# First norm of a hybrid layer: context's norm, scales and softplus queue issued behind the image's, first head's value products ahead of the context's products

## The chip, the cores and the metric

The kernel runs on one core of a Trainium2 chip. The metric is the device time of one execution in microseconds (us), here the median over runs. The engines are TensorE (PE, with its weight loads as PEld), VectorE (DVE), ScalarE (ACT), GpSimd (POOL) and SyncE (SP), which issues the DMAs.

## What is computed

One layer over 512 image tokens and 256 context tokens of 1024 channels. The part in question is its start:

```python
sc, scc = silu(c), silu(c_ctx)
mod_x = sc @ mod_w + mod_b            # shift, scale, gate: image
mod_c = scc @ mod_w + mod_b           # the same for the context
hx = modulate(rms_norm(x, norm1_g), sh1x, sc1x)
hc = modulate(rms_norm(ctx, norm1_g), sh1c, sc1c)
px, pc = split_proj(hx @ w_in), split_proj(hc @ w_in)
ret_c, ret_x = retention_mixer(pc, px, ret_decay, rows)      # 4 heads, q, k of 128, v of 256
lru_c, lru_x = lru_mixer(pc[4], px[4], conv_w, conv_b, lru_wa, lru_ba, lru_wx, lru_bx, lru_lambda)
```

The retention needs log_sigmoid(ret_decay) and the recurrent mixer softplus(-lru_lambda). After it come gates, an output projection, a second norm, a feed-forward over 16384 single-neuron experts and a last norm; the change does not touch them.

## The kernel before

Channels lie on the 128 partitions in eight chunks k, tokens in the free dimension: xT is the image (8 chunks of 128x512), cT the context (128x256). A float32 product is made of three products of rounded parts (mm3, L63 to 67: L65 is high by high, L66 and L67 take one low part each); split (L60 to 62) makes the parts, the high one on ACT, the low one on DVE. In names an h or l at the end is the high or low part.

The first norm, L169 to 284. inv_rms (L174) squares the chunks on ACT, adds them up on DVE (ssq), sums over the partitions by one product with ones, and takes scale, root and reciprocal (L184 to 186). The shift and scale of a chunk k come from mod_rows1 (L198; PE, eight products of 256 columns and two transposes, for image and context at once) where k is below NROW = 4, and otherwise from mod_dots (L210; DVE, two products of 128x1024 with crow, for the image, and two more later for the context). normed (L218) makes xn on DVE, the high part hh or ch on ACT and the low part hl or cl on DVE. The image's chunks go in the order of KORD, and with each, PE adds its share to four projections: outs0 = pu, p5, pk, pq, of which pu and pk have 768 columns (image and context) in a slot of 1024, p5 and pq 512. PSUM has three slots of 1024 and two of 512, and these are all of it: whatever comes later waits until a slot is read out. Then stand in the program the softplus queue (L245 to 277: 24 columns, some 30 small DVE operations), the context's mod_dots, norm and chunks.

Head 0 follows. Context products of pu (proj_ctx), lru_in (L301 to 321: u from pu by ACT and six DVE taps, x5 from p5 and its gelu g5), context products of pk, rope_split of pk and pq; lru_scan (L324: four gate products pg, their tanh as roots or gi on ACT, then exp, tanh, square, root and the scans on DVE); and in head() the value products pv (six token tiles t, each 24 products of 256 columns), their mean vm and the parts vh and vl (L411 to 426), and scores pS, weights P and outputs po (L428 to 443). A head has two recurrent chunks: the second's pu and p5 come behind the first's lru_scan.

The order in which an engine takes its instructions is fixed when the program is built, by a scheduler that goes by readiness on its own model and by the order in the source; a slot of a pool that is still in use makes the next user wait for the last reader.

Of the kernel before, what the change touches and what calls it, by code (L numbers as in the profile page):

```python
# [44 lines left out]
NROW = 4  # L45
# [7 lines left out]
def block_kernel(ctx: ExitStack, tc: tile.TileContext, A):  # L53
# [118 lines left out]
    rstd = st.tile([128, NT], F32, name="rstd")  # L172

    def inv_rms(src, o, n):  # L174
        ps = psum(n if n == NX else D, name="ps_ss")
        ssq = st.tile([128, NX], F32, name="ssq")
        S.activation(ssq[:, :n], src[:, 0], AF.Square)
        for k in range(1, KT):
            sq = st.tile([128, NX], F32, name="sq", bufs=2)
            S.activation(sq[:, :n], src[:, k], AF.Square)  # L180
            V.tensor_tensor(ssq[:, :n], ssq[:, :n], sq[:, :n], op=OP.add)
        PE.matmul(ps[:, :n], onesf, ssq[:, :n], start=True, stop=True)
        r = rstd[:, o:o + n]
        V.tensor_scalar(r, ps[:, :n], 1.0 / D, EPS, op0=OP.mult, op1=OP.add)  # L184
        S.activation(r, r, AF.Sqrt)
        V.reciprocal(r, r)


    def mod_load(k):
        if k < NROW:  # L190
            mw = st.tile([128, KT, 256], F32, name="mw", bufs=2)
            SY.dma_start(mw, A["mod_a"][k])
        else:
            mw = st.tile([128, 2, D], F32, name="mwc", bufs=4)
            SY.dma_start(mw, A["mod_c"][k - NROW])
        return mw
# [53 lines left out]
    sp_z = const.tile([128, 24], F32, name="sp_z")  # L250
    sp_q = const.tile([128, 24], F32, name="sp_q")
    S.activation(sp_w, spin, AF.Abs)
    S.activation(sp_w, sp_w, AF.Exp, scale=-1.0)
    V.tensor_scalar(sp_z, sp_w, 2.0, None, op0=OP.add)
    V.reciprocal(sp_z, sp_z)
    V.tensor_tensor(sp_z, sp_z, sp_w, op=OP.mult)
    V.tensor_tensor(sp_q, sp_z, sp_z, op=OP.mult)
    V.memset(sp, 1.0 / 19)
    for n in range(8, -1, -1):
        V.tensor_tensor(sp, sp, sp_q, op=OP.mult)  # L260
        V.tensor_scalar(sp, sp, 1.0 / (2 * n + 1), None, op0=OP.add)
    V.scalar_tensor_tensor(sp, sp, 2.0, sp_z, op0=OP.mult, op1=OP.mult)
    V.tensor_scalar(sp_w, spin, -1.0, 0.0, op0=OP.mult, op1=OP.max)
    V.tensor_tensor(sp, sp, sp_w, op=OP.add)
    sp4 = const.tile([128, 16], F32, name="sp4")
    V.tensor_scalar(sp4, sp[:, 0:16], 4.0, None, op0=OP.mult)
    nsp4 = const.tile([128, 16], F32, name="nsp4")
    V.tensor_scalar(nsp4, sp[:, 0:16], -4.0, None, op0=OP.mult)
    hb = const.tile([128, 32], F32, name="hb")
    V.tensor_scalar(hb, col("ba", 0, 32), 0.5, None, op0=OP.mult)  # L270
    epsc = const.tile([128, 1], F32, name="epsc")
    V.memset(epsc, EPS)
    lgam = const.tile([128, 8], F32, name="lgam")
    V.tensor_scalar(lgam, sp[:, 16:24], -1.0, None, op0=OP.mult)
    nlgam = sp[:, 16:24]
    lg768 = const.tile([128, 4], F32, name="lg768")
    V.tensor_scalar(lg768, lgam[:, 4:8], 768.0, None, op0=OP.mult)
# [776 lines left out]
```

## Time and profile before

| | us |
|---|---|
| median of 3 runs (1873.9 to 1877.84) | 1876.19 |
| profiled execution, its own time | 1879.51 |
| its span | 1877.7 |
| PE busy (97% of the span) | 1820.2 |
| DVE busy (81%) | 1512.3 |
| ACT busy (44%) | 824.3 |
| mean granted clock of PE | 0.99 |

Busy time is the sum of an engine's instructions in the one profiled execution; a wait is idle time just before an instruction, put down to what ended it. A granted clock of 1.00 is 2.4 GHz, 0.50 is 1.2 GHz. In names of the views digits of buffers are left out: p is p5.

### The profile page before, as it was taken

How to read it: one execution, taken by the hardware profiler on the slowest of the kernel's cores; microseconds unless marked ns; L12 is line 12 of the kernel's file. 1: busy time of each engine (PE TensorE's matmuls, PEld its weight loads, DVE VectorE, ACT ScalarE, POOL GpSimd, SP SyncE). 2: the span in 40 equal slices, each digit the busy share in tenths (PEclk: the TensorE clock that was granted, in tenths of full speed). 3: DMA queues.
4: the chain of work that ended last, by engine and by line, in shares of the span. 5: the costliest groups of instructions: out<-in, count | busy, mean ns of one | idle time of the engine just before them, and what ended most of it. 6: DMA issues, size and time to landing. Idle time of an engine off the chain costs nothing.

```text
span 1877.7 us, 26999 instructions
## 1 busy us (share of the span) xinstructions
PE 1820.2 (97%) x9969; PEld 1603.0 (85%) x9969; DVE 1512.3 (81%) x2801; ACT 824.3 (44%) x1213; POOL 375.7 (20%) x327
## 2 busy tenths in 40 slices
PE   7899999999999999999999999999999999999997
PEld 3788888887888989999999988888887888888885
DVE  8987878788844579999988578886786879788688
ACT  4667575765222444445545333333333333333333
POOL 0000000000000000000022134443443535445350
PEclk9999999999999999999999999999999999999999
DMA  7122121225943433567778999998989999999986
GB/s 310 52 67 68 57 68 57 68 64 189 335 136 115 138 108 115 184 193 238 261 283 299 317 345 328 345 336 298 323 324 312 346 340 337 347 331 355 319 302 208
DMA packets 175753, 432.72 MB, mean 230 GB/s; under 512 B 14082, under 2 KB 87170, under 8 KB 171140
## 3 DMA queue, kind: packets, MB, share of 16 engines
q1 hardware_dynamic: 138756, 296.75, 46.7%
q0 software_dynamic: 36864, 134.23, 19.7%
q8 instruction: 78, 1.28, 0.3%
q14 instruction: 55, 0.45, 0.1%
HBM read 389.32 MB, written 41.62 MB: 229 GB/s over the span
## 4 chain that ended last, share of the span: by engine, by line
PE 74%; DVE 11%; DMA 9%; ACT 3%; issue 2%; SPq 1%; DVEq 0%; ACTq 0%
PE po L65 8%; PE po L66 8%; PE po L67 8%; PE pS L65 7%; PE pS L66 7%; PE pS L67 7%; DMA wt<-wd 4%; DMA vw<-in_v_dram 2%; DVE wl L62 2%; PE pgm L65 1%; PE pgm L66 1%; PE pgm L67 1%; PE pmm L66 1%; PE pmm L67 1%; PE pmm L65 1%
## 5 line engine op out<-in xcount | busy, mean ns | idle before, releaser
L61 ACT ACTIVATE wh<-w 128x1024 fp32r<-128x1024 f32 (+1 forms) x216 | 224.8, 1043 | 369.0 <-DMA w<-in_uT_dram 105.0
L65 PE MATMUL pS<-h2h,wh 128*128 128x384 f32 x1024 | 347.1, 339 | 7.0 <-ACT gt L756 6.7
L67 PE MATMUL pS<-h2h,wl 128*128 128x384 f32 x1024 | 346.1, 338 | 0.7 <-DVE wl L62 0.7
L66 PE MATMUL pS<-h2l,wh 128*128 128x384 f32 x1024 | 346.2, 338 | 0.0
L62 DVE TENSOR_TENSOR wl<-w,wh 128x1024 fp32r<-128x1024 f32 (+1 forms) x216 | 259.0, 1200 | 88.2 <-ACT wh L61 87.5
L801 POOL DMA_INDIRECT row<-in_u_dram,ei x128 | 181.9, 1421 | 609.7 <-DVE row L803 316.0
L66 PE MATMUL po<-vwl,ah 128*128 128x512 f32 x768 | 299.9, 391 | 1.2 <-DVE vwl L62 1.2
L67 PE MATMUL po<-vwh,al 128*128 128x512 f32 x768 | 298.9, 390 | 0.0
L65 PE MATMUL po<-vwh,ah 128*128 128x512 f32 x768 | 271.5, 395 | 10.0 <-ACT vwh L61 8.1
L61 ACT ACTIVATE ah<-af 128x384 fp32r<-128x384 f32 x128 | 67.2, 525 | 387.0 <-PE po L66 220.2
L809 POOL DMA_INDIRECT row<-in_v_dram,ei x128 | 183.9, 1436 | 208.5 <-DVE acc L814 175.2
L65 PEld LDWEIGHTS pS<-h2h,wh 128*128 128x128 f32 x1024 | 193.2, 189 | 14.3 <-ACT gt L756 8.4
L67 PEld LDWEIGHTS pS<-h2h,wl 128*128 128x128 f32 x1024 | 193.1, 189 | 6.0 <-DVE wl L62 1.0
L66 PEld LDWEIGHTS pS<-h2l,wh 128*128 128x128 f32 x1024 | 193.3, 189 | 4.3
L62 DVE TENSOR_TENSOR vwl<-vw,vwh 128x1024 fp32r<-128x1024 f32 x128 | 156.1, 1220 | 27.1 <-ACT vwh L61 25.6
L65 PEld LDWEIGHTS po<-vwh,ah 128*128 128x128 f32 x768 | 143.1, 188 | 38.4 <-ACT vwh L61 10.6
L814 DVE SCALAR_TENSOR_TENSOR acc<-row,act,acc 128x1024 f32<-128x1024 f32 x127 | 162.7, 1281 | 14.0 <-DMA row<-in_v_dram,ei 13.4
L66 PEld LDWEIGHTS po<-vwl,ah 128*128 128x128 f32 x768 | 144.4, 188 | 29.9 <-DVE vwl L62 2.3
L67 PEld LDWEIGHTS po<-vwh,al 128*128 128x128 f32 x768 | 144.4, 188 | 27.8 <-DVE al L62 0.2
L61 ACT ACTIVATE vwh<-vw 128x1024 fp32r<-128x1024 f32 x128 | 134.4, 1051 | 61.6 <-DMA vw<-in_v_dram 59.9
L803 DVE SCALAR_TENSOR_TENSOR row<-row,h2t 128x1024 f32<-128x1024 f32 x128 | 153.8, 1220 | 2.4 <-DMA row<-in_u_dram,ei 2.4
L62 DVE TENSOR_TENSOR al<-af,ah 128x384 fp32r<-128x384 f32 x128 | 71.0, 554 | 62.6 <-ACT ah L61 57.5
(372 smaller groups left out, 3505.8 us busy)
## 6 DMA issues: line engine op xcount, KB each, us to landing
w<-in_uT_dram SPq DMA_DIRECT2D x128, 512.0 KB
vw<-in_v_dram SPq DMA_DIRECT2D x128, 512.0 KB
w<-in_w_in_dram SPq DMA_DIRECT2D x48, 512.0 KB
wd<-stg SPq DMA_DIRECT2D x24, 1024.0 KB
modb<-in_mod_t_dram SPq DMA_DIRECT2D x32, 512.0 KB
wt<-wd SPq DMA_DIRECT2D x9, 1536.0 KB
gd<-gt SPq DMA_DIRECT2D x57, 192.0 KB
gr<-gd SPq DMA_DIRECT2D x57, 192.0 KB
```

Source lines behind the costliest of these rows:

```text
L61: S.activation(hi, src, AF.Copy)
L62: V.tensor_tensor(lo, src, f(hi), op=OP.subtract)
L65: PE.matmul(out, wh, xh, start=start, stop=False)
L66: PE.matmul(out, wh, xl, start=False, stop=False)
L67: PE.matmul(out, wl, xh, start=False, stop=stop)
L801: G.indirect_dma_start(out=row, out_offset=None, in_=A["u"], in_offset=bass.IndirectOffsetOnAxis(ap=ei[:, j:j + 1], axis=0))
L803: V.scalar_tensor_tensor(row, row, 1.0, h2t, op0=OP.mult, op1=OP.mult, accum_out=act[:, j:j + 1])
L809: G.indirect_dma_start(out=row, out_offset=None, in_=A["v"], in_offset=bass.IndirectOffsetOnAxis(ap=ei[:, j:j + 1], axis=0))
L814: V.scalar_tensor_tensor(acc, row, act[:, j:j + 1], acc, op0=OP.mult, op1=OP.add)
```

## The change

NROW is 3: chunk 3 too gets its shift and scale by dot products. The norm's sum of squares is done on PE alone, eight products with a matrix of 1/1024 for each source, and the root takes its epsilon as a bias; the image's sum lies in p5's bank, the context's in pu's last 256 columns. All the loads of the modulation and of cT are issued early. outs0 and pv0, a slot of 1024 columns for the first four value tiles, are taken at the start, and the row products lie in pv0 and pk for the time. Head 0's value weights are loaded and split early. With issue_after, the context's norm, scales and chunks are put behind the image's last normed, the softplus queue behind the context's last. The value products of the image (t = 0 to 3, in pv0) stand ahead of the context's products of pu and pk, and those of the context (t = 4 and 5, in the last 256 columns of pk and of pu) behind them. In head 0 the values are read out (vm, vh, vl) ahead of lru_scan.

```diff
--- before.py
+++ after.py
@@ -42,7 +42,7 @@
 SPILL, RING = 57, 9
 GFIRST, GSTEPS, SSTEPS = 10, 252, 124
 AHEAD = 2
-NROW = 4
+NROW = 3
 TORD = (0, 1, 3, 2)
 HG = 4
 WG = 16
@@ -64,7 +64,7 @@
     def mm3(out, wh, wl, xh, xl, start, stop):
         PE.matmul(out, wh, xh, start=start, stop=False)
         PE.matmul(out, wh, xl, start=False, stop=False)
-        PE.matmul(out, wl, xh, start=False, stop=stop)
+        return PE.matmul(out, wl, xh, start=False, stop=stop)
 
     const = ctx.enter_context(tc.tile_pool(name="const", bufs=1, reuse_waits="tile"))
     hp = ctx.enter_context(tc.tile_pool(name="hp", bufs=1, reuse_waits="tile"))
@@ -95,7 +95,8 @@
     for h in range(4):
         c = 2 * h
         plan += [A["w_in"][16 + c], A["w_in"][24 + c], A["w_in"][4 + h], A["w_in"][h], A["gate_w"][c],
-                 A["w_v"][h, :, 0:4], A["w_v"][h, :, 4:8], A["w_in"][17 + c], A["w_in"][25 + c], A["gate_w"][c + 1],
+                 *([A["w_v"][h, :, 0:4], A["w_v"][h, :, 4:8]] if h else []),
+                 A["w_in"][17 + c], A["w_in"][25 + c], A["gate_w"][c + 1],
                  *(A["w_in"][32 + 8 * g + c] for c, g in early if h == 3),
                  A["w_in"][8 + 2 * h], A["w_in"][9 + 2 * h]]
     for c in range(KT):
@@ -170,28 +171,27 @@
     for k in range(0, KT, 4):
         SY.dma_start(xT[:, k:k + 4], A["xT"][:, k:k + 4])
     rstd = st.tile([128, NT], F32, name="rstd")
-
-    def inv_rms(src, o, n):
-        ps = psum(n if n == NX else D, name="ps_ss")
-        ssq = st.tile([128, NX], F32, name="ssq")
-        S.activation(ssq[:, :n], src[:, 0], AF.Square)
-        for k in range(1, KT):
-            sq = st.tile([128, NX], F32, name="sq", bufs=2)
+    epsc = const.tile([128, 1], F32, name="epsc")
+    V.memset(epsc, EPS)
+    meanD = st.tile([128, 128], F32, name="meanD")
+    V.memset(meanD, 1.0 / D)
+
+    def inv_rms(src, o, ps):
+        n = src.shape[2]
+        for k in range(KT):
+            sq = st.tile([128, NX], F32, name="sq", tag="xn", bufs=3)
             S.activation(sq[:, :n], src[:, k], AF.Square)
-            V.tensor_tensor(ssq[:, :n], ssq[:, :n], sq[:, :n], op=OP.add)
-        PE.matmul(ps[:, :n], onesf, ssq[:, :n], start=True, stop=True)
-        r = rstd[:, o:o + n]
-        V.tensor_scalar(r, ps[:, :n], 1.0 / D, EPS, op0=OP.mult, op1=OP.add)
-        S.activation(r, r, AF.Sqrt)
-        V.reciprocal(r, r)
+            PE.matmul(ps, meanD, sq[:, :n], start=k == 0, stop=k == KT - 1)
+        S.activation(rstd[:, o:o + n], ps, AF.Sqrt, bias=epsc)
+        V.reciprocal(rstd[:, o:o + n], rstd[:, o:o + n])
 
 
     def mod_load(k):
         if k < NROW:
-            mw = st.tile([128, KT, 256], F32, name="mw", bufs=2)
+            mw = st.tile([128, KT, 256], F32, name="mw", bufs=5)
             SY.dma_start(mw, A["mod_a"][k])
         else:
-            mw = st.tile([128, 2, D], F32, name="mwc", bufs=4)
+            mw = st.tile([128, 2, D], F32, name="mwc", tag="mw", bufs=5)
             SY.dma_start(mw, A["mod_c"][k - NROW])
         return mw
 
@@ -216,72 +216,96 @@
         V.scalar_tensor_tensor(scal1[:, k, s:s + 1], m[:, 1, s:s + 1], 1.0, col("n1g", k), op0=OP.add, op1=OP.mult)
 
     def normed(src, n, s, k, h_, l_):
-        xn = st.tile([128, NX], F32, name="xn", bufs=2)
+        xn = st.tile([128, NX], F32, name="xn", tag="xn", bufs=3)
         shift = mod1[:, k, 0, s:s + 1]
         V.scalar_tensor_tensor(xn[:, :n], src[:, k], scal1[:, k, s:s + 1], rstd[:, s * NX:s * NX + n], op0=OP.mult, op1=OP.mult)
         S.activation(h_[:, k], xn[:, :n], AF.Identity, bias=shift)
-        V.scalar_tensor_tensor(l_[:, k], xn[:, :n], shift, f(h_[:, k]), op0=OP.add, op1=OP.subtract)
-
-    inv_rms(xT, 0, NX)
-    KORD = (0, 4, 1, 2, 5, 6, 3, 7)
-    mws = {0: mod_load(0)}
+        return V.scalar_tensor_tensor(l_[:, k], xn[:, :n], shift, f(h_[:, k]), op0=OP.add, op1=OP.subtract)
+
+    outs0 = [psum(n, name=nm) for nm, n in (("pu", NT), ("p5", NX), ("pk", NT), ("pq", NX))]
+    pv0 = psum(D, name="pv0")
+    inv_rms(xT, 0, outs0[1])
+    KORD = tuple(range(KT))
+    mws = {0: mod_load(0), 1: mod_load(1)}
     prefetch(2)
+    mws[2], mws[3], mws[4] = (mod_load(k) for k in (2, 3, 4))
     prefetch(4)
-    for k in KORD[1:]:
+    for k in range(NROW):
+        mod_rows1(k, mws[k], (pv0[:, :512], pv0[:, 512:], outs0[2][:, 512:])[k])
+    for k in range(5, KT):
         mws[k] = mod_load(k)
+    SY.dma_start(cT, A["cT"])
     first = [ahead.pop(0) for _ in range(4)]
-    for k in range(2):
-        mod_rows1(k, mws[k], psum(name="pr"))
-    outs0 = [psum(n, name=nm) for nm, n in (("pu", NT), ("p5", NX), ("pk", NT), ("pq", NX))]
+    wv0 = []
+    for i in range(2):
+        w = wst.tile([128, 4, 256], F32, name="w", tag="w")
+        SY.dma_start(w, A["w_v"][0, :, 4 * i:4 * i + 4])
+        wv0.append([st.tile([128, 4, 256], F32R, name=f"wv{m}", bufs=2) for m in "hl"])
+        split(*wv0[i], w)
     for k in KORD:
-        if 1 < k < NROW:
-            mod_rows1(k, mws[k], psum(D, name="pr"))
-        elif k >= NROW:
+        if k >= NROW:
             mod_dots(k, mws[k], 0)
-        normed(xT, NX, 0, k, hh, hl)
+        x_done = normed(xT, NX, 0, k, hh, hl)
         for out, (wh, wl) in zip(outs0, first):
-            mm3(out[:, :NX], wh[:, k], wl[:, k], hh[:, k], hl[:, k], k == KORD[0], k == KORD[-1])
-
-    spin = const.tile([128, 24], F32, name="spin")
-    V.tensor_copy(spin[:, 0:16], col("lam", 0, 16))
-    SY.dma_start(spin[:, 16:24], A["rd"].to_broadcast([128, 8]))
-    sp = const.tile([128, 24], F32, name="sp")
...
-    for k in range(NROW, KT):
-        mod_dots(k, mws[k], 1)
-    SY.dma_start(cT, A["cT"])
-    inv_rms(cT, NX, NC_)
-    for k in range(KT):
-        normed(cT, NC_, 1, k, ch, cl)
+            mm = mm3(out[:, :NX], wh[:, k], wl[:, k], hh[:, k], hl[:, k], k == KORD[0], k == KORD[-1])
+
+    def values(out, t, wv):
+        th, tl, o = (hh, hl, 128 * t) if t < 4 else (ch, cl, 128 * t - NX)
+        for k in range(KT):
+            mm = mm3(out, th[:, k, o:o + 128], tl[:, k, o:o + 128], wv[k // 4][0][:, k % 4], wv[k // 4][1][:, k % 4], k == 0, k == KT - 1)
+        return mm
+
+    with tc.issue_after(x_done.ins):
+        inv_rms(cT, NX, outs0[0][:, NT:])
+
+    for t in range(4):
+        with tc.issue_after(mm.ins):
+            mm = values(pv0[:, 256 * t:256 * t + 256], t, wv0)
+    with tc.issue_after(x_done.ins):
+        for k in KORD:
+            if k >= NROW:
+                mod_dots(k, mws[k], 1)
+            c_done = normed(cT, NC_, 1, k, ch, cl)
+            for i in (0, 2):
+                wh, wl = first[i]
+                mm = mm3(outs0[i][:, NX:NT], wh[:, k], wl[:, k], ch[:, k], cl[:, k], k == 0, k == KT - 1)
+    pvc = [outs0[i][:, NT:] for i in (2, 0)]
+    with tc.issue_after(c_done.ins):
+
+        spin = const.tile([128, 24], F32, name="spin")
+        V.tensor_copy(spin[:, 0:16], col("lam", 0, 16))
+        SY.dma_start(spin[:, 16:24], A["rd"].to_broadcast([128, 8]))
+        sp = const.tile([128, 24], F32, name="sp")
...
+    for t in (4, 5):
+        with tc.issue_after(mm.ins):
+            mm = values(pvc[t - 4], t, wv0)
     sstk.close()
     eg = front.enter_context(tc.tile_pool(name="eg", bufs=1, reuse_waits="tile", side="right"))
     lru = mid.tile([128, KT, NX], F32, name="lru", tag="m0")
@@ -408,20 +432,24 @@
 
         vh = rp.tile([128, 6, 256], F32R, name="vh")
         vl = rp.tile([128, 6, 256], F32R, name="vl")
-        wv = [wtile() for i in range(2)]
+        wv = [wtile() for i in range(2)] if h else None
         for t2 in range(3):
-            pv = psum(name="pv")
-            for tt in range(2):
-                t = 2 * t2 + tt
-                for k in range(KT):
-                    th, tl, o = (hh, hl, 128 * t) if t < 4 else (ch, cl, 128 * t - NX)
-                    mm3(pv[:, 256 * tt:256 * tt + 256], th[:, k, o:o + 128], tl[:, k, o:o + 128],
-                        wv[k // 4][0][:, k % 4], wv[k // 4][1][:, k % 4], k == 0, k == KT - 1)
+            if h:
+                pv = psum(name="pv")
+                for tt in range(2):
+                    values(pv[:, 256 * tt:256 * tt + 256], 2 * t2 + tt, wv)
+                pv = pv.rearrange("p (a b) -> p a b", a=2)
+            elif t2 < 2:
+                pv = pv0[:, 512 * t2:512 * t2 + 512].rearrange("p (a b) -> p a b", a=2)
             vm = rp.tile([128, 2], F32, name="vm", bufs=2)
-            V.tensor_reduce(vm, pv.rearrange("p (a b) -> p a b", a=2), axis=AX.X, op=OP.add)
+            if h or t2 < 2:
+                V.tensor_reduce(vm, pv, axis=AX.X, op=OP.add)
+            else:
+                for tt in range(2):
+                    V.tensor_reduce(vm[:, tt:tt + 1], pvc[tt], axis=AX.X, op=OP.add)
             V.tensor_scalar(vm, vm, -1.0 / 256, None, op0=OP.mult)
             for tt in range(2):
-                t, src = 2 * t2 + tt, pv[:, 256 * tt:256 * tt + 256]
+                t, src = 2 * t2 + tt, pv[:, tt] if h or t2 < 2 else pvc[tt]
                 S.activation(vh[:, t], src, AF.Identity, bias=vm[:, tt:tt + 1])
                 V.scalar_tensor_tensor(vl[:, t], src, vm[:, tt:tt + 1], f(vh[:, t]), op0=OP.add, op1=OP.subtract)
         yield
@@ -496,9 +524,7 @@
             next(hd)
             if h == 0:
                 pu, pp, pk, pq = outs0
-                proj_ctx(pu, *first[0])
                 li = lru_in(0, pu, pp)
-                proj_ctx(pk, *first[2])
             else:
                 pu, pp, pk, pq = psum(NT, name="pu"), psum(name="p5"), psum(NT, name="pk"), psum(name="pq")
                 proj(pu, *wtile(), ctx_too=True)
@@ -507,8 +533,11 @@
                 proj(pk, *wtile(), ctx_too=True)
                 proj(pq, *wtile())
             hd.send((pk, pq))
+            if h == 0:
+                next(hd)
             lru_scan(2 * h, *li)
-            next(hd)
+            if h:
+                next(hd)
             pu, pp = psum(NT, name="pu"), psum(name="p5")
             proj(pu, *wtile(), ctx_too=True)
             proj(pp, *wtile())
```

On PE, in head 0 before: between the value products of the first two token tiles (pv) and of the next two stand the four gate products pg of chunk 0.

```order
L66 MATMUL pv<-wl,hh 128x256
L67 MATMUL pv<-wh,hl 128x256
L65 MATMUL pg<-uh,wh 128x512 [waits Activation_49]
L65 MATMUL pg<-uh,wh 128x512 [waits DVE_49,PE_49]
L66 MATMUL pg<-ul,wh 128x512 [waits DVE_49]
L67 MATMUL pg<-uh,wl 128x512
L65 MATMUL pg<-uh,wh 128x256
...
L67 MATMUL pg<-uh,wl 128x256
L65 MATMUL pv<-wh,hh 128x256 [waits DVE_49]
L66 MATMUL pv<-wl,hh 128x256
```

And now, from the last value product of the context (in pu) on; p_928 is p5 of chunk 1, for which 24 products precede the first pg, and the last row is pu of chunk 1.

```order
L67 MATMUL pu<-wvh,cl 128x256
L65 MATMUL p_928<-hh,wh 128x512 [waits Activation_49]
L66 MATMUL p_928<-hl,wh 128x512
L67 MATMUL p_928<-hh,wl 128x512 [waits DVE_49]
...
L65 MATMUL pg<-uh,wh 128x512 [waits DVE_49,PE_49]
L66 MATMUL pg<-ul,wh 128x512
...
L65 MATMUL pg<-uh,wh 128x512 [waits Activation_49]
...
L65 MATMUL pg<-uh,wh 128x512 [waits Activation_49]
...
L65 MATMUL pg<-uh,wh 128x512 [waits DVE_49]
...
L65 MATMUL pu<-hh,wh 128x512 [waits Activation_49]
```

The value products have gone ahead of u; between two pg there is now nothing else, and each pg's first product waits.

On ACT, in head 0 before, from the first tanh of a gate (roots) to the third's:

```order
L335 ACTIVATE roots<-pg,hb 128x768 [waits PE_49]
L335 ACTIVATE gi<-pg,hb 128x768 [waits PE_49]
L364 ACTIVATE rx<-pq 128x512 [waits DVE_49]
L341 ACTIVATE a<-roots,nsp_450 128x768 [waits Activation_49]
L335 ACTIVATE roots<-pg,hb 128x768 [waits PE_49]
L61 ACTIVATE wh<-w 128x1024 [waits DMAHW0_49,PE_49]
L342 ACTIVATE roots<-roots,sp_448 128x768 [waits Activation_49]
```

And now, from the first to the second of the first direction, and on to the second gi:

```order
L359 ACTIVATE roots<-pg,hb 128x768 [waits PE_49]
L419 ACTIVATE dt_772<-dist,lg_692,sp 128x320 [waits Pool_49]
L420 ACTIVATE sc<-dist,lgam 128x320
L365 ACTIVATE a<-roots,nsp_686 128x768 [waits Activation_49]
L419 ACTIVATE dt_778<-dist,lg_692,sp 128x320 [waits Pool_49]
L420 ACTIVATE sc<-dist,lgam 128x320
L388 ACTIVATE rx<-pk 128x512 [waits DVE_49]
L61 ACTIVATE kh<-pk 128x256
L366 ACTIVATE roots<-roots,sp_684 128x768 [waits Activation_49]
L367 ACTIVATE q<-a 128x768
L359 ACTIVATE gi<-pg,hb 128x768 [waits PE_49]
```

Nine instructions (decay tables dt and sc, a, the copy rx of pk, kh, a tanh and q) now stand between the first gate's tanh roots and the second's, gi.

On DVE now, from u's taps to the last vl of the early values (pv_137 is pv0):

```order
L334 SCALAR_TENSOR_TENSOR u<-pu,cols,u 128x511 [waits DVE_49]
...
L334 SCALAR_TENSOR_TENSOR u<-pu,cols,u 128x255 [waits DVE_49]
L454 SCALAR_TENSOR_TENSOR vl<-pv_137,vm,vh 128x256 [waits Activation_49]
L446 TENSOR_REDUCE vm<-pv_137 128x2
L343 TENSOR_TENSOR g_798<-g_798,x_796 128x512 [waits DVE_49]
...
L449 TENSOR_REDUCE vm<-pu 128x1 [waits DVE_49]
L62 TENSOR_TENSOR ul<-u,uh 128x768 [waits Activation_49]
L450 TENSOR_SCALAR vm<-vm 128x2 [waits DVE_49]
...
L62 TENSOR_TENSOR wl<-w,wh 128x1024 [waits DMAHW0_49,PE_49,Activation_49]
L345 SCALAR_TENSOR_TENSOR g_798<-g_798,x_796 128x512 [waits Activation_49]
...
L454 SCALAR_TENSOR_TENSOR vl<-pv_137,vm,vh 128x256 [waits Activation_49]
...
L454 SCALAR_TENSOR_TENSOR vl<-pv_137,vm,vh 128x256 [waits Activation_49]
```

The four vl are mixed with u's taps, the steps of g, ul, a weight's split and the end of the softplus queue, which stood ahead of the context's chunks before.

## Rows read from the trace of the kernel before

**Rows 1.** The page, parts 1 and 4: busy time by engine, and the chain.

```profile
PE 1820.2 (97%) x9969; PEld 1603.0 (85%) x9969; DVE 1512.3 (81%) x2801; ACT 824.3 (44%) x1213; POOL 375.7 (20%) x327
...
PE 74%; DVE 11%; DMA 9%; ACT 3%; issue 2%; SPq 1%; DVEq 0%; ACTq 0%
```

**Rows 2.** Waits of PE, 60 to 215 us: us in total, times, longest.

```profile
PE pg L65 <- ACT uh L61: 2.8, 1, 2.8
PE pS L65 <- ACT x L315: 1.5, 2, 0.8
PE pv L66 <- DVE wl L62: 0.5, 1, 0.5
```

**Rows 3.** Stretches of PE: length, busy time (instructions), granted clock, DMA share, GB/s.

```profile
30.00:40.00 10.00, 8.66 (x25) 0.66 0.71 294
67.19:73.05 5.86, 5.86 (x49) 1.00 0.60 186
82.53:90.15 7.62, 7.62 (x26) 0.58 0.00 0
90.15:164.50 74.35, 73.50 (x393) 1.00 0.20 61
109.84:115.31 5.47, 5.47 (x27) 1.00 0.30 95
```

**Rows 4.** Timeline of PE: start, us, engine, line, operation [idle before].

```profile
6.03 7.19 PE L167 MATMUL crow<-c,sel 2*128 2x512 f32 x8 [6.03 <-DVE c L159]
...
30.50 0.52 PE L65 MATMUL pu<-hh,wh 128*128 128x512 f32 x1 [4.24 <-ACT hh L222]
...
47.58 3.62 PE L200 MATMUL pr<-mw,scol 128*2 128x256 f32 x16 [0.75 <-DVE mod L206]
...
67.19 0.28 PE L65 MATMUL pu<-ch,wh 128*128 128x256 f32 x1
...
82.53 1.22 PE L65 MATMUL pg<-uh,wh 128*128 128x512 f32 x2 [2.82 <-ACT uh L61]
...
164.51 0.28 PE L65 MATMUL pk<-ch,wh 128*128 128x256 f32 x1
```

**Rows 5.** Timeline of ACT at 74 us.

```profile
74.38 0.98 ACT L303 ACTIVATE u<-pu,cols 128x768 f32<-128x768 f32 x1
```

**Rows 6.** Lines of DVE by form, 20 to 135 us: busy us, mean ns | idle before.

```profile
L214 DVE SCALAR_TENSOR_TENSOR mscr<-mwc,m 128x1024 f32<-128x1024 f32 x16 | 19.4, 1215 | 0.0
L62 DVE TENSOR_TENSOR wl<-w,wh 128x1024 fp32r<-128x1024 f32 x10 | 12.2, 1220 | 2.4 <-ACT wh L61 2.3
...
L223 DVE SCALAR_TENSOR_TENSOR hl<-xn,mod,hh 128x512 fp32r<-128x512 f32 x8 | 5.7, 736 | 0.0
...
L186 DVE RECIPROCAL rstd<-rstd 128x512 f32<-128x512 f32 x1 | 3.3, 3346 | 0.0
L310 DVE SCALAR_TENSOR_TENSOR u<-pu,cols,u 128x511 f32<-128x511 f32 x4 | 3.0, 743 | 0.0
...
L426 DVE SCALAR_TENSOR_TENSOR vl<-pv,vm,vh 128x256 fp32r<-128x256 f32 x6 | 2.9, 476 | 0.0
```

**Rows 7.** Lines of ACT by form, 60 to 135 us, the same columns.

```profile
L341 ACT ACTIVATE a<-roots,nsp 128x768 f32<-128x768 f32 x4 | 4.1, 1022 | 0.0
L342 ACT ACTIVATE roots<-roots,sp 128x768 f32<-128x768 f32 x4 | 4.1, 1022 | 0.0
...
L343 ACT ACTIVATE q<-a 128x768 f32<-128x768 f32 x4 | 3.3, 836 | 0.0
...
L395 ACT ACTIVATE dt<-dist,lg,sp 128x320 f32<-128x320 f32 x2 | 1.3, 646 | 0.2 <-POOL dist L378 0.2
...
L396 ACT ACTIVATE sc<-dist,lgam 128x320 f32<-128x320 f32 x2 | 1.1, 554 | 1.2 <-POOL dist L378 1.2
...
L364 ACT ACTIVATE rx<-pk 128x512 f32<-128x512 f32 x1 | 0.6, 576 | 0.0
L61 ACT ACTIVATE kh<-pk 128x256 fp32r<-128x256 f32 x1 | 0.4, 372 | 0.0
```

More of the change, by code (lines that the diff above doesn't have):

```diff
@@ L240, in block_kernel @@
             mod_dots(k, mws[k], 0)
-        normed(xT, NX, 0, k, hh, hl)
+        x_done = normed(xT, NX, 0, k, hh, hl)
         for out, (wh, wl) in zip(outs0, first):
-            mm3(out[:, :NX], wh[:, k], wl[:, k], hh[:, k], hl[:, k], k == KORD[0], k == KORD[-1])
-    spin = const.tile([128, 24], F32, name="spin")
-    V.tensor_copy(spin[:, 0:16], col("lam", 0, 16))
-    SY.dma_start(spin[:, 16:24], A["rd"].to_broadcast([128, 8]))
-    sp = const.tile([128, 24], F32, name="sp")
-    sp_w = const.tile([128, 24], F32, name="sp_w")
@@ L250, in block_kernel @@
[L250 to L277, printed above, removed]
-    for k in range(NROW, KT):
-        mod_dots(k, mws[k], 1)
-    SY.dma_start(cT, A["cT"])
-    inv_rms(cT, NX, NC_)
-    for k in range(KT):
-        normed(cT, NC_, 1, k, ch, cl)
+            mm = mm3(out[:, :NX], wh[:, k], wl[:, k], hh[:, k], hl[:, k], k == KORD[0], k == KORD[-1])
@@ new lines, in block_kernel @@
+    with tc.issue_after(x_done.ins):
[12 more added lines that the diff above has]
+        sp = const.tile([128, 24], F32, name="sp")
+        sp_w = const.tile([128, 24], F32, name="sp_w")
+        sp_z = const.tile([128, 24], F32, name="sp_z")
+        sp_q = const.tile([128, 24], F32, name="sp_q")
+        S.activation(sp_w, spin, AF.Abs)
+        S.activation(sp_w, sp_w, AF.Exp, scale=-1.0)
+        V.tensor_scalar(sp_z, sp_w, 2.0, None, op0=OP.add)
+        V.reciprocal(sp_z, sp_z)
+        V.tensor_tensor(sp_z, sp_z, sp_w, op=OP.mult)
+        V.tensor_tensor(sp_q, sp_z, sp_z, op=OP.mult)
+        V.memset(sp, 1.0 / 19)
+        for n in range(8, -1, -1):
+            V.tensor_tensor(sp, sp, sp_q, op=OP.mult)
+            V.tensor_scalar(sp, sp, 1.0 / (2 * n + 1), None, op0=OP.add)
+        V.scalar_tensor_tensor(sp, sp, 2.0, sp_z, op0=OP.mult, op1=OP.mult)
+        V.tensor_scalar(sp_w, spin, -1.0, 0.0, op0=OP.mult, op1=OP.max)
+        V.tensor_tensor(sp, sp, sp_w, op=OP.add)
+        sp4 = const.tile([128, 16], F32, name="sp4")
+        V.tensor_scalar(sp4, sp[:, 0:16], 4.0, None, op0=OP.mult)
+        nsp4 = const.tile([128, 16], F32, name="nsp4")
+        V.tensor_scalar(nsp4, sp[:, 0:16], -4.0, None, op0=OP.mult)
+        hb = const.tile([128, 32], F32, name="hb")
+        V.tensor_scalar(hb, col("ba", 0, 32), 0.5, None, op0=OP.mult)
+        lgam = const.tile([128, 8], F32, name="lgam")
+        V.tensor_scalar(lgam, sp[:, 16:24], -1.0, None, op0=OP.mult)
+        nlgam = sp[:, 16:24]
+        lg768 = const.tile([128, 4], F32, name="lg768")
+        V.tensor_scalar(lg768, lgam[:, 4:8], 768.0, None, op0=OP.mult)
```

## The prediction

> **What bounds the kernel now.** I read the page's busy times first: TensorE (PE) is busy 97% of the span and is 74% of the chain [rows 1]. So a change at the start counts only by what it moves on PE. Next I took the waits of PE over the first head, 60 to 215 us. There are three, 4.8 us together [rows 2]: before the first gate product, twice before scores, once in the value products. Then the stretches: from 82.53 to 90.15 PE has a granted clock of 0.58 (1.2 GHz for most of it) after the 2.82 us wait, and from 90.15 to 164.50 it never waits [rows 3]. The timeline gives the marks [rows 4]: image products from 30.50 (after an idle 4.24) to 67.19, where the context's products begin; first gate product pg at 82.53; and at 164.51 the context product of pk in head 1. From there on PE has the same order in both programs, so the sum is the shift of that row. I name E the moment in the new program where the last context value product ends.
>
> Prices on PE at full clock: 48 products of 256 columns took 5.86 us, 0.12 each; 24 of 512 took 5.47, 0.23 each [rows 3].
>
> **The change part by part.**
>
> *Image part.* PE now sums the squares itself. The crow products end at 13.2 (6.03 + 7.19) [rows 4]; eight meanD products of 512 columns in plain f32, three k of row products and 16 transposed values follow. A row product of 256 columns in f32 costs 3.62/8 = 0.45 at full clock [rows 4], so 512 columns cost 0.9, and twice that at half clock, which PE had here up to about 20 us. Three norms at 1.8, eight row products, three norms, 14 row products, two norms: 30.8. Then ACT takes the square root (0.6), and DVE the reciprocal, 3.35 [rows 6]: 34.8. Two weight splits wl stand behind it on DVE, 2 x 1.22 less overlap [rows 6]: 37.1; first xn and hh: first image product at 38.4 where it was 30.5. After that DVE no longer has the context's ten dot products (10 x 1.2, less two for the additional k), the ssq additions and the softplus queue between its xn and hl, so the stream of hl keeps ahead of PE after the first two k: last hl at 57.9. 96 products at 0.235 and 3 us of waits for the first two hl put the end at 63.8, against 67.19: **-3.4** (from -7, if PE is at full clock from the start, to -1, if half clock lasts longer).
>
> *Context's norm.* Its eight products are added to PE, 8 x 0.45 less a last overlap: **+3.5**. The one product that they replace lay inside the image part, and is out of that sum already.
>
> *Values before context.* The 96 value products of the image take 11.5 us of PE and need nothing but hh, hl and w_v, which are there. They cover what DVE now does late: ten mscr, eight xn and cl. By DVE's order the last cl is done at about 81.7; PE wants it at 83.9. So I cost the late context scales at nothing; without this cover they would be some 12 us of wait. These products were done later before: moved, not added. E comes out at 90.4.
>
> *Waits that go.* The 2.8, the 0.5 and about half of the scores' 1.5, 0.7 (the other half comes back in point 6) [rows 2]. Chunk 0's gate products at half clock go too: the 24 of them (12 of 512 and 12 of 256 columns, 4.2 us at full clock) took 7.6 from 82.53 to 90.15 [rows 3], 3.4 more. Together **-7.4**; the bounds are -4 (if half clock comes back elsewhere) and -8.2.
>
> *New waits behind E.* Before, 48 + 48 value products stood between chunk 0's gates and chunk 1; now nothing does, and PE meets ACT and DVE. The waits are in the program; their sizes I work out along the orders of ACT and DVE.
> 1. p5 of chunk 1 waits for x5, which stands on ACT behind u; u reads pu, whose second bank the last context values write. 0.98 [rows 5] and a copy of 128x512 like rx, 0.58 [rows 7]: 1.6.
> 2. pg of gate 0 takes the PSUM slot of the early values and waits for the fourth vl. On DVE stand before it, from u at E+1.2: six taps (0.74 and 0.48), four vl, two sums, three steps of g and ul, a weight split, and some ten softplus steps of 0.17. With the overlap of 0.08 between two [rows 6] that is E+11.3. PE has p5 until E+7.2 (1.6 + 24 x 0.235): 4.1.
> 3. pg 1 waits for the tanh of pg 0, 0.9, and 0.1 of passing: 1.0.
> 4. pg 2 waits for the tanh gi of pg 1. On ACT nine instructions stand before it: 0.65, 0.55, 1.02, 0.65, 0.55, 0.58, 0.37, 1.02, 0.84 [rows 7], 6.2 less eight overlaps of 0.1, 5.4; then gi, 0.9. PE's pg 1 itself takes 1.05: 5.1.
> 5. pg 3 waits for the vl of the context's values in pk: 1.8 by DVE's order.
> 6. The third score pS waits for its P on DVE behind the roots, scans and lru of chunk 0: 4.1.
> 7. P, Ph, Pl and pS alternate with less work between, and uh of chunk 1: 2.5.
>
> Together **+20.2**. No row of the old trace shows these waits, so I bound them. The lower end is 14: points 1 to 4, which rest on the order of the program and on durations read above, make 11.8, and 2 are left for the rest. The upper end is 24, if DVE loses the whole of its small steps on the way. I take the middle sum: the nearest row is the wait of 2.8 for uh [rows 2], which came up although PE had value products to do between u and the gates, and now it has fewer there.
>
> A row on point 1: u began 1.2 us after the last context product into pu (73.2 to 74.38 [rows 5]). The Trainium skill, page "PSUM — Partial Sum Buffer", section on bank collisions, asks that PSUM be guarded by bank and not by address; this speaks against values in columns beside pu's own. Were columns enough, u could start 5.8 us sooner, and points 1 and 2 would nearly vanish: the sum would be about +7. The semaphores of the new program do wait for the bank.
>
> Sum: -3.4 + 3.5 - 7.4 + 20.2 = **+12.9 us**. The profiled execution takes 1879.51 us (span 1877.7 and 1.8 around it), which gives 1892.4. The median of the three runs shown is 1876.19, 3.3 below the profiled one; the shift set on it is **1889.1 us**. The bounds of the terms give 1879 to 1895.
>
> **The rivals.**
>
> *Faster, 1868.9.* The values are pure cover, and ACT and DVE keep up behind E: terms -3.4, +3.5, -7.4 alone. For it: from 90.15 to 164.50 PE never waited, so the chains of ACT and DVE are not far behind [rows 3]. Against: it had 96 value products and the pu of chunk 1 as cover there. It is decided by whether pg 0 starts within about 1 us of the end of p5: the fourth vl would have to be there by E+8, three us sooner than DVE's list allows. Chance 0.14.
>
> *No change, about 1877.* The image part gains its 7, the waits come at the lower end of 14: -7 + 3.5 - 7.4 + 14 = +3, or less. Chance 0.10.
>
> *Slower still, about 1895.* After the waits of points 1 and 2 PE is granted half clock again, as it was after the waits of 4.24 us (0.66 in 30 to 40 us) and 2.82 us (0.58) [rows 3]. If that begins at the wait of 1.6 us, p5 takes 11.2 us and not 5.6, pg 0 starts at about E+13 with its own 2 us twice as long, and what follows shifts by some 6 us in all: 1895. The Trainium skill, page "TensorE: Matmul & The Clock Gate", part 1, says that the clock falls when the engine is little busy and comes back when it is kept busy; the rows agree, and by it this rival would need more idling than one wait of 1.6. Chance 0.2.
>
> **How the numbers follow.** The forecast of +12.9 with its bounds has 0.56, the slower rival 0.2, no change 0.10, faster 0.14. 0.2% is 3.75 us, about what a measurement of this kernel can tell. Faster 0.14, the same 0.12 (the rival and the low edge of the forecast), slower 0.74. The range 1874 to 1897 leaves out the faster rival and little else; the likeliest case alone is 1879 to 1895.
>
> **What would show it.** First image product at about 38 us and image products over at 64; context's norm and the values without a wait up to E near 90; then waits of PE on x5, vl, roots and gi in the first gates, some 12 us, and 6 to 8 more before head 1's pk, which comes near 177. Waits under 8 us in all behind E, or a first context product that waits for ch or cl, would prove me wrong, in opposite directions.

## The result, and the profile after

The changed kernel takes 1894.64 us in the median of six runs (1891.74 to 1904.32), the kernel before 1876.65 beside it: ratio 1.0104, 95% interval 1.0081 to 1.0128. It is 18.0 us slower by the medians. The two profiled executions (1894.9 and 1879.51) differ by 15.4, their spans by the same.

The page's busy times and chain after; against [rows 1] the share of PE is the same, and it is busy for 7.5 us more:

```profile
PE 1827.7 (97%) x9979; PEld 1609.6 (85%) x9979; DVE 1510.5 (80%) x2797; ACT 820.3 (43%) x1208; POOL 372.6 (20%) x327
...
PE 77%; DVE 10%; DMA 8%; ACT 3%; issue 1%; SPq 0%; DVEq 0%; ACTq 0%
```

Waits of PE from 60 to 215 us, to be held against [rows 2]:

```profile
PE pg L65 <- DVE vl L454: 5.1, 2, 4.4
PE pg L65 <- ACT gi L359: 3.8, 1, 3.8
PE pS L65 <- DVE P L465: 3.2, 2, 2.7
PE p L65 <- ACT x L339: 1.6, 1, 1.6
PE pg L65 <- ACT roots L359: 1.0, 1, 1.0
PE po L66 <- DVE Pl L62: 0.7, 1, 0.7
```

The waits for uh and wl are gone, as is that of the scores for x5; in their place stand 15.4 us of waits for vl, gi, P, x5 (now at p5 of chunk 1), roots and Pl. The timeline of PE, the marks of [rows 4], with the first product of p5 of chunk 1, of each gate, and of pk's context part in head 1:

```profile
37.90 0.50 PE L65 MATMUL pu<-hh,wh 128*128 128x512 f32 x1 [2.81 <-ACT hh L222]
...
77.44 0.28 PE L65 MATMUL pu<-ch,wh 128*128 128x256 f32 x1
...
90.69 0.50 PE L65 MATMUL p<-hh,wh 128*128 128x512 f32 x1 [1.57 <-ACT x L339]
...
100.84 0.77 PE L65 MATMUL pg<-uh,wh 128*128 128x512 f32 x1 [4.41 <-DVE vl L454]
...
104.09 0.80 PE L65 MATMUL pg<-uh,wh 128*128 128x512 f32 x1 [0.99 <-ACT roots L359]
...
110.18 0.80 PE L65 MATMUL pg<-uh,wh 128*128 128x512 f32 x1 [3.80 <-ACT gi L359]
...
113.14 0.80 PE L65 MATMUL pg<-uh,wh 128*128 128x512 f32 x1 [0.66 <-DVE vl L454]
...
179.70 0.28 PE L65 MATMUL pk<-ch,wh 128*128 128x256 f32 x1
```

The image's products begin 7.4 us later than before, the context's 10.25. From the context's first product to the end of its values PE does not wait. Then u, on ACT (the row of [rows 5], 14.8 us later):

```profile
89.16 0.99 ACT L327 ACTIVATE u<-pu,cols 128x768 f32<-128x768 f32 x1 [4.54 <-PE pu L67]
```

Stretches of PE behind that, columns as in [rows 3]:

```profile
90.69:100.84 10.15, 5.74 (x24) 0.96 0.13 36
100.84:118.00 17.16, 11.70 (x33) 0.52 0.04 16
128.72:140.00 11.28, 10.08 (x29) 0.70 0.14 46
140.00:185.00 45.00, 45.00 (x225) 1.00 0.17 53
```

p5 runs at full clock (5.7 us busy); the four gates and the first products behind them have a granted clock of 0.52, 1.2 GHz nearly throughout; a second stretch of it lies at 128 to 140 us. From 140 to 185 us PE is not idle at all. The context product of pk in head 1 comes at 179.70, 15.2 us after its place before. From that row on the traces hold 9278 products of PE in both programs, and they take 1713.4 us now and 1713.2 before: in the two profiled executions the whole loss lies ahead of it.

### The profile page after: what moved, and what is told of

Its sections match the earlier page's. It is cut to its first block, busy times and chain, and to the rows that moved or that the text cites. A ratio compares the mean times of both kernels' runs of the same rounds, so it can differ in the third digit from the quotient of the medians.

```text
span 1893.1 us, 26998 instructions
## 1 busy us (share of the span) xinstructions
PE 1827.7 (97%) x9979; PEld 1609.6 (85%) x9979; DVE 1510.5 (80%) x2797; ACT 820.3 (43%) x1208; POOL 372.6 (20%) x327
## 4 chain that ended last, share of the span: by engine, by line
PE 77%; DVE 10%; DMA 8%; ACT 3%; issue 1%; SPq 0%; DVEq 0%; ACTq 0%
PE po L65 8%; PE po L66 8%; PE po L67 8%; PE pS L65 7%; PE pS L66 7%; PE pS L67 7%; DMA vw<-in_v_dram 3%; DMA wt<-wd 2%; DVE wl L62 2%; PE pgm L65 1%; PE pgm L66 1%; PE pgm L67 1%; PE pmm L66 1%; PE pmm L67 1%; PE pmm L65 1%
## 5 line engine op out<-in xcount | busy, mean ns | idle before, releaser
L843 DVE SCALAR_TENSOR_TENSOR acc<-row,act,acc 128x1024 f32<-128x1024 f32 x127 | 162.5, 1280 | 16.5 <-DMA row<-in_v_dram,ei 15.8
```

Of the source, the lines that this page charges most:

```text
L843: V.scalar_tensor_tensor(acc, row, act[:, j:j + 1], acc, op0=OP.mult, op1=OP.add)
```

## The experiments

Behind that row the trace of every kernel below has the same 9278 products of PE, and the profiled executions take 1705 to 1723 us for them, a scatter that was not traced further and that the ratios carry. So the readings go by the row ("pk") and by the start of u (chunk 0), and the ratios, each against runs of the kernel before on its chip, stand beside them. Each pk comes from one profiled execution, and how far it moves from one execution to the next was not measured; only the image's reciprocal can be compared, and in the four kernels with the same start (changed, x1, x3, x4) it begins within 0.3 us. The columns on PE split the time from 0 to pk into busy and idle; busy time at half clock counts in full.

| kernel | u starts | pk | pk against before | PE busy to pk | PE idle to pk | ratio to before (95%) |
|---|---|---|---|---|---|---|
| before | 74.4 | 164.5 | | 146.1 | 18.4 | |
| changed | 89.2 | 179.7 | +15.2 | 154.3 | 25.4 | 1.0104 (1.0081 to 1.0128) |
| x1_values_back | 81.3 | 180.3 | +15.8 | 152.5 | 27.9 | 1.0097 (1.0080 to 1.0114) |
| x2_early_readout | 88.2 | 177.6 | +13.1 | 151.9 | 25.7 | 1.0101 (1.0072 to 1.0129) |
| x3_softplus_early | 89.4 | 176.4 | +11.9 | 150.9 | 25.5 | 1.0062 (1.0045 to 1.0078) |
| x4_x5_first | 89.2 | 177.4 | +12.9 | 154.0 | 23.4 | 1.0086 (1.0064 to 1.0109) |
| y1_norm_only | 82.3 | 171.8 | +7.2 | 150.5 | 21.2 | 1.0040 (1.0021 to 1.0059) |
| y2_before_late | 89.1 | 186.0 | +21.5 | 150.0 | 36.0 | 1.0139 (1.0117 to 1.0161) |
| y3_values_only | 89.4 | 175.3 | +10.8 | 149.3 | 26.0 | 1.0064 (1.0037 to 1.0091) |
| y4_three_repairs | 90.7 | 174.4 | +9.8 | 152.0 | 22.4 | 1.0039 (1.0023 to 1.0055) |
| z1_norm_alone | 87.0 | 176.3 | +11.8 | 154.9 | 21.4 | 1.0068 (1.0045 to 1.0090) |
| z2_loads_alone | 80.4 | 169.1 | +4.6 | 139.5 | 29.7 | 1.0068 (1.0043 to 1.0094) |
| z3_after_old_norm | 86.0 | 171.1 | +6.6 | 145.7 | 25.4 | 1.0040 (1.0020 to 1.0060) |
| z4_values_old_norm | 89.2 | 176.1 | +11.5 | 145.5 | 30.6 | 1.0086 (1.0057 to 1.0115) |

### Is it the place of the values?

x1_values_back:

```diff
-    for t in range(4):                 # and t = 4, 5 behind the context
-        with tc.issue_after(mm.ins):
-            mm = values(pv0[:, 256 * t:256 * t + 256], t, wv0)
...
+            pv = psum(name="pv")       # in head 0 as in the others
+            for tt in range(2):
+                values(pv[:, 256 * tt:256 * tt + 256], 2 * t2 + tt, wv)
```

> The changed kernel with head 0's value products, their weights' load and split and their read-out put back to where they were (behind the first gates, in slots of their own); the norm on PE, NROW 3, and the late context scales and softplus queue stay. My theory: the loss lies behind the context values, where the moved products no longer cover ACT and DVE. Then the waits of the first gates on vl, roots and gi (9.9 us) go, the first context product waits some 8 us for ch or cl since nothing covers the late scales, and the time is 1878 to 1886, with the context product of pk in head 1 near 168 us instead of 179.7. Rival: the norm on PE and the late context work are the loss, wherever the values stand: 1890 or more, pk near 177.

My theory fell here, and the rival's time came, with pk even later than its 177. The waits of the gates on vl, roots and gi went, but pk stayed where it was, +15.8. Without the cover PE waits for the context, then 2.3 us for the late softplus queue at a gate, and later for the scores' qh, which the order of ACT now brings late:

```profile
PE pS L65 <- ACT qh L61: 7.4, 1, 7.4
PE pu L65 <- ACT ch L221: 4.8, 1, 4.8
```

So putting the values back repairs nothing while the context's work is late: what it saves at the gates comes back as these waits.

### Is it the slot, the softplus steps, or x5?

x2_early_readout, x3_softplus_early and x4_x5_first, one edit each of the changed kernel:

```diff
+        if h == 0:                     # x2: at the head of head(0)
+            for t2 in range(2):
+                readout(pv0[:, 512 * t2:512 * t2 + 512].rearrange("p (a b) -> p a b", a=2), t2)
...
-    with tc.issue_after(c_done.ins):   # x3: ahead of the context's chunks
+    with tc.issue_after(x_done.ins):
         spin = const.tile([128, 24], F32, name="spin")
...
+        S.activation(x5, pp, AF.Copy)  # x4: x5 and g5 ahead of u
...
         S.activation(u, pu[:, :NT], AF.Identity, scale=col("conv_w", 16 + c), bias=col("conv_b", c))
...
-        S.activation(x5, pp, AF.Copy)
```

> The changed kernel with the means and parts vm, vh, vl of the image's values read out of their PSUM slot ahead of u, while the context's products run (vh and vl of four tiles in a pool that is open then; the ones matrix and a scale of the root stand for the matrix of 1/1024). Theory A: the PSUM slot of the early values is what holds the gates. Then pg 0 starts right behind p5 of chunk 1, near 96.5 us and not 100.8, the half clock in the gates goes too, and the time falls by 8 to 12 us, to 1883 to 1887. Theory B: the chain of ACT and DVE from u on is the bound and the slot only the place where it shows: pg 1 to pg 3 and the scores wait for what is saved at pg 0, and the time falls by under 3 us.

> The changed kernel with the softplus queue put ahead of the context's scales and chunks. My theory: its small steps among the taps and vl cost DVE about 2 us ahead of the fourth vl, and ahead of the context's chunks they cost as much there: pg 0 starts 1 to 2 us sooner against a context that is 0 to 2 us later, time 1892 to 1895. Rival: the queue's new place is the main loss: the fourth vl comes by 97 us, the waits at the gates fall by 4 or more, time 1888 or less.

> The changed kernel with x5 and its gelu g5 issued ahead of u in lru_in. My theory: the wait of p5 of chunk 1 for x5 (1.6 us) goes, but pg 0 still waits for the fourth vl behind u and the context's last values, so what is saved there is lost at pg 0: time 1893 to 1895, wait at pg 0 up from 4.4 to about 6. Rival: the wait of 1.6 is a loss of its own: 1893 falls by all of it, and the half clock at the gates gets shorter: 1887 to 1892.5.

x2 did what it should at its place: no wait for vl is left, and the second gate begins at 97.72 us. But pk came only 2.1 us sooner than in the changed kernel, and the ratio did not move. Theory B: what is saved at the slot is waited for behind it, at roots and gi, and at qh and ql of the scores:

```profile
PE pS L65 <- ACT qh L61: 4.0, 1, 4.0
PE pS L66 <- DVE ql L62: 2.9, 1, 2.9
PE pg L65 <- ACT roots L357: 2.8, 2, 1.8
PE pu L65 <- ACT gi L357: 1.7, 1, 1.7
...
PE pg L65 <- ACT gi L357: 1.3, 1, 1.3
```

x3 moved pk by 3.3 us, more than my 0 to 2, but not by the rival's way: the wait for the fourth vl grew from 4.4 to 7.7 and those for roots and gi went. PE is idle as long as in the changed kernel (25.5 and 25.4 us to pk); what x3 saves is busy time, because behind one long wait the gates follow each other without a gap and PE is at full clock again after one and a half of them (products of 512 columns take 0.63 us at first and 0.40 then). x4: the wait for x5 went, the wait at pg 0 rose to 6.3 as expected, pk came 2.3 us sooner; the ratio is within the interval of the changed kernel. Then the three at once.

> The changed kernel with the three repairs of the runs before at once: values read out ahead of u, softplus queue ahead of the context's chunks, x5 ahead of u. By theory U u still starts at 88 to 90, and what the repairs save at the gates is only in part given back at the scores: pk of head 1 at 172 to 176, time 1885 to 1889, still above the kernel before by 8 us or more. Theory S (the slot, the softplus steps and x5 are the loss, each hidden by the others): pk at 168 or less, time 1881 or less.

pk at 174.4, theory U's range; the ratio 1.0039 leaves 7 us of loss. No single wait of these three was the cause: each hid the next.

### The parts of the change, one by one

y1_norm_only takes x1 and no longer holds the context's work back; y3_values_only does the same with the values in their new place; y2_before_late puts this one part into the kernel before:

```diff
-    for k in range(NROW, KT):          # y2, in the kernel before
-        mod_dots(k, mws[k], 1)
-    inv_rms(cT, NX, NC_)
...
+    with tc.issue_after(x_done.ins):
+        inv_rms(cT, NX, NC_)
+        for k in range(KT):
+            if k >= NROW:
+                mod_dots(k, mws[k], 1)
+            c_done = normed(cT, NC_, 1, k, ch, cl)
+    with tc.issue_after(c_done.ins):   # the softplus queue
```

> The values in their old place, and the context's norm, scales and softplus queue no longer held behind the image's: of the change only the norm on PE, NROW 3 and the early loads are left. Theory D (late work: what is lost is the time in which DVE stood idle before the image's root, and the later start of u that follows): u starts within 4 us of the 74.4 of before, the context product of pk in head 1 comes at 162 to 168 us, time 1874 to 1881. Theory N (the norm on PE with its eight products more is a loss by itself): pk at 170 or later, time 1883 or more.

> The kernel before, with one part of the change alone: the context's norm, scales and chunks behind the image's last chunk, and the softplus queue behind the context's. Norm and values as before. Theory D: DVE idles in the first 30 us as in the changed kernel, the first context product waits, u starts 5 to 10 us later, and pk of head 1 comes at 172 to 182: time 1885 to 1894. Theory V (the values ahead of u are the loss, and late context work is covered by them when they can run first): pk within 3 us of 164.5, time 1874 to 1880.

> The changed kernel with the context's norm, scales and softplus queue no longer held back: the values ahead of the context's products stay, with the norm on PE. Theory D in its narrow form (DVE's lateness is the whole loss): DVE is ahead, the fourth vl comes in time, pk of head 1 within 5 us of 164.5, time under 1882. Theory U (whatever puts u later takes cover away behind it): u starts at 88 to 90 as in the changed kernel, because PE is busy until then, the waits behind it come to 8 us or more, and pk lies at 172 to 178, time 1885 to 1891.

Each of the three costs. y2 is the worst of all kernels, beyond the range given: u at 89.1, with PE waiting for the context's norm and its first chunk:

```profile
PE ps_ss L182 <- DVE mod L215: 7.1, 1, 7.1
PE pu L65 <- ACT ch L222: 4.8, 1, 4.8
```

The direction is theory D's, but DVE does not stand idle early: in the first 30 us it is as busy as before (22.5 and 21.7 us), and it is idle later (5.9 us busy from 40 to 60 us, 20.0 before).

In y3 u starts at 89.4, as in the changed kernel, because PE is busy until then; pk is at +10.8, theory U, with two waits carrying it:

```profile
PE pg L65 <- DVE vl L452: 7.7, 1, 7.7
PE po L66 <- DVE Pl L62: 4.6, 1, 4.6
```

y1 was to be at 164.5 +- 4 by theory D and at 170 or more by theory N: it is at 171.8. That was new to me, and the last four runs take the norm apart.

```diff
...
-            PE.matmul(ps, meanD, sq[:, :n], start=k == 0, stop=k == KT - 1)
-        S.activation(rstd[:, o:o + n], ps, AF.Sqrt, bias=epsc)
...
+            V.tensor_tensor(ssq[:, :n], ssq[:, :n], sq[:, :n], op=OP.add)
+        PE.matmul(ps, onesf, ssq[:, :n], start=True, stop=True)
...
+        V.tensor_scalar(r, ps, 1.0 / D, EPS, op0=OP.mult, op1=OP.add)
+        S.activation(r, r, AF.Sqrt)
```

(z2, z3 and z4; z1 is the reverse, in the kernel before.)

> The kernel before with the norm's sums alone on PE (eight products for each source, root with a bias); NROW 4, loads, context's work and values as before. Theory N (the norm on PE puts the image's root behind crow and the row products, so DVE stands idle before it and all that DVE has to do comes later): the image's reciprocal starts at 28 to 32 us and not at 18.2, u at 78 to 84, pk of head 1 at 169 to 174, time 5 to 9 us over before. Theory L (the loads' order and NROW 3 are what y1_norm_only lost): pk within 3 us of 164.5, time within 4 us of before.

> The mirror of the run before it: NROW 3, the loads' order and the PSUM places of the changed kernel, with the squares summed on DVE and one product with ones as before; context's work and values as before. Theory N: reciprocal at 18 to 21 us, pk of head 1 at 161 to 167, time within 4 us of before on either side. Theory L: pk at 169 or later, 5 us or more over before.

> The changed kernel with the squares summed on DVE and one product, as before; the rest of the change stays. Theory N: the image's part ends 3 to 6 us sooner, u starts at 83 to 87 and not at 89.2, pk of head 1 at 172 to 176 and not at 179.7: time 4 to 8 us under the changed kernel. Theory U alone (the order of values and u decides, the norm is neutral as I had forecast it): pk at 178 to 181, time within 3 us of the changed kernel.

> Of the change the values ahead of the context's products (with the early loads that they need), the squares summed on DVE, context's norm, scales and softplus queue not held back. Theory U: PE is through with image, values and context at 82 to 86, u starts then, 8 to 12 us later than before, and ACT and DVE give PE too little behind it: pk of head 1 at 168 to 173, time 4 to 8 us over before. Theory C (the values are harmless when DVE has its work done): pk at 166 or less, time within 3 us of before.

z1 shows the norm's price by itself: pk +11.8, above the range given. The image's root comes as late as theory N says. Its reciprocal, 18.21 us before, starts in z1 and in the changed kernel at

```profile
31.73 3.35 DVE L187 RECIPROCAL rstd<-rstd 128x512 f32<-128x512 f32 x1 [0.23 <-ACT rstd L186]
```

```profile
30.87 3.35 DVE L186 RECIPROCAL rstd<-rstd 128x512 f32<-128x512 f32 x1 [0.88 <-ACT rstd L185]
```

and with the old sums in the changed kernel (z3) at

```profile
20.50 3.35 DVE L189 RECIPROCAL rstd<-rstd 128x512 f32<-128x512 f32 x1 [0.43 <-ACT rstd L188]
```

z3 is the largest single repair of the changed kernel: pk 8.6 us sooner, at 171.1, earlier even than theory N's 172 to 176. DVE's busy time in the first two stretches, before:

```profile
0.00:20.00 20.00, 12.68 (x24) 1.00 0.90 356
20.00:30.00 10.00, 9.05 (x20) 1.00 0.94 369
```

changed:

```profile
0.00:20.00 20.00, 5.59 (x13) 1.00 0.89 355
20.00:30.00 10.00, 5.58 (x14) 1.00 0.94 376
```

and z3:

```profile
0.00:20.00 20.00, 11.14 (x22) 1.00 0.90 359
20.00:30.00 10.00, 9.57 (x18) 1.00 0.91 365
```

From 0 to 30 us DVE does 11.2 us of work in the changed kernel, 21.7 before. The sums that it no longer has make up 5.4 to 6 of the difference; the other 4.5 to 5 are idle time before an image root that comes 12.7 us later, and from 40 to 60 us DVE is full in either kernel (10.0 and 9.7 of 10 us in the changed one), so they are not made up there.

That idle time of DVE is not what the price mainly consists of, though. PE from 0 to pk, columns as in [rows 3], in the kernel before, z1, z3 and the changed kernel:

```profile
0.00:164.51 164.51, 146.09 (x692) 0.96 0.36 130
0.00:176.29 176.29, 154.92 (x720) 0.96 0.33 122
0.00:171.11 171.11, 145.67 (x674) 0.92 0.34 125
0.00:179.70 179.70, 154.30 (x702) 0.92 0.33 120
```

From before to z1, 8.8 of the 11.8 us are busy time of PE and 3.0 idle time; from z3 to the changed kernel all 8.6 are busy time. With the norm's products PE is busy for 2.8 us before, 1.7 in z3, 14.3 in z1 and 14.4 in the changed kernel: sixteen float32 products stand on the engine that is busy nearly throughout where two did. So by this account the norm's price is in the main its own time on PE; that DVE's later start adds to it is not shown.

z2, the mirror, does not come out at zero: +4.6 and a ratio of 1.0068, theory L's numbers; there PE waits 7.8 us for the context's ssq on DVE. Its profiled execution is the fastest of its six runs; where the rest of the 11.7 us between the medians lies, its one trace does not show. So the norm on PE costs, and the loads' order with NROW 3 costs too, and together (y1, +7.2) they cost less than the norm alone (z1, +11.8): from z2 to y1 PE is busy for 11.1 us more but idle for 8.5 less, since the wait for ssq goes. How z2's share divides between loads, NROW and the order of the chunks (KORD, now 0 to 7 in turn) stays open. z4 goes theory U's way, but beyond its ranges: u at 89.2 (82 to 86 expected), pk at 176.1 (168 to 173); and y3, the same with the norm on PE, has pk at 175.3.

The parts do not add. The norm on PE costs 11.8 in the kernel before, 2.6 from z2 to y1, nothing from z4 to y3 (-0.8) and 8.6 from z3 to the changed kernel. The late context costs 8.6 with the values in their old place (y1 to x1) and 4.4 with them ahead (y3 to the changed kernel), and with the old norm and the values ahead it gains 4.9 (z4 to z3). None of the twelve beats the kernel before.

## Why the prediction was right

*The sum.* I had forecast +12.9, with 1874 to 1897; it is +18.0 by medians and +15.4 by profiled executions, of which the row of pk shows 15.2. The direction, the place and most of the terms held. The bounds of the terms, added up, are +2.3 and +22.5, 1879 and 1899; the prediction puts the upper one at 1895.

*Image part, -3.4.* Its products end at 62.5, -4.7. First product at 37.9 (38.4 forecast), reciprocal from 30.87 to 34.2 (34.8). The norm's image products took 1.76 us each up to 18.5 us and 0.95 from 22 us on, as priced. The prediction's sum to 30.8 does not come out of its terms, which with 14 row products at 0.45 make 33.0; the trace has 14 instructions of 0.23 there, half products, and the norm's last product ends at 30.1.

*Context's norm, +3.5, values as cover, 0.* From 62.5 to the first context product at 77.44 lie 14.9 us: 11.5 of values and 3.4 of norm, and no wait for ch or cl. E came at 89.1 (90.4).

*New waits, +20.2.* In order: x5 1.57 (1.6), fourth vl 4.41 (4.1), roots 0.99 (1.0), gi 3.80 (5.1), vl of the context 0.66 (1.8), P 2.66 (4.1), the rest 1.2 (2.5): 15.3 together, near the lower bound of 14. The first six are there, in the order given, and of the seventh P and Pl, but no wait for uh; the chain of nine ACT instructions and DVE's list were read rightly, and the later waits were sized too long.

*Waits that go, -7.4.* This is the step that failed. I took 3.4 us of gates at half clock for gone. They came back larger: the 24 gate products take 8.9 us where full clock gives 4.2, five products of pu and fourteen of scores and outputs from 130.78 to 137.70 us add 4.0 (2.1 against 1.2, and 6.3 against 3.2), 8.7 us in all. That is the rival "slower still", which I gave 0.2, with another beginning: the 1.57 us wait did not bring the clock down (p5 ran at 2.4 GHz), the 4.41 before pg 0 did. The Trainium skill's page "TensorE: Matmul & The Clock Gate", part 1, says that the clock follows how busy the engine has been. The trace agrees: PE is busy without a gap at full clock from 62.5 us to 89.1, and for 14.4 of the 25 us from 90 to 115, in which the clock falls.

So -1.3 at E, -4.9 of waits and +8.7 of clock turn 12.9 into 15.4, against 15.2 of the row. That the sum came this near is partly luck: waits sized too long stood against a clock term with the wrong sign.

*What the forecast did not see* is how the parts hang together. It compared the image part with the one before and found it a little shorter, and so put the norm down as neutral (-3.4 and +3.5). z3 shows 8.6 us of the 15.2 to hang on it, with the values ahead and the context late beside it; of these, 3.2 are there when u starts. Split by what PE did, the 15.2 are 7.0 of idle time and 8.2 of busy time, the busy part being the norm's products and the half clock, less the row products that NROW 3 saves. And the list of waits behind E was right as a list, but x2 and x4 show that the entries tried are not worth their length: take one away, and the next grows.

*The bank rule.* u did wait for the last value product in pu's second bank (89.16, right behind it). That is the guard by bank that the page "PSUM — Partial Sum Buffer" of the Trainium skill, section on bank collisions, asks for; it is a semaphore of the program, and no run here reads pu while its second bank is written. In the prediction's row on the kernel before, 73.2 is the end of pk's last context product; pu's own ended at 72.97, 1.4 us ahead of u. The estimate of +7 with the columns free was not tried: all of PSUM is taken there, and x2, which took away the larger wait that hangs on it, gave 2.1.

## What to carry to other kernels

Where one engine is busy nearly throughout, look for the chain on the others that feeds its next stage, and ask of each moved piece of work whether it delays the head of that chain; here every kernel started u later than before and lost, though not by as much as u was late (x1: u 6.9 us later, pk 15.8; y3: 15.0 and 10.8). What is put on the busy engine itself costs its own time there, unless it takes a wait away: the norm's products cost 11.8 us in z1 and 2.6 from z2 to y1. Work that is off the path at one place can fill an idle engine there for nothing (the context's dot products before the image's root), and costs when it is moved behind. A list of waits tells where time is lost but not what removing one gives: take the entries away one at a time and together, and look at the clock beside them: x3 kept the sum of the waits and gained 3.3 us.

## What was not expected of the hardware

A wait of 1.57 us before p5 left PE at full clock, but in x2 the waits of 0.99, 1.34 and 1.81 us ahead of the second, third and fourth gate, none of them much longer, ended with the clock down: the first products of the second and third took 0.50 us, that of the fourth 0.80. So it was down after several such waits in a row, where a single one had not brought it down.
